# Token mixing in a two-block transformer: four edits to when side work is issued between the projections

## The chip, the cores and the metric

The kernel runs on one core of one Trainium2 chip. The time is device microseconds (us) of one execution; the kernel before was run three times, with a median of 1366.09 us (1365.25 to 1366.57). One further execution was profiled, and all rows below come from it.

## The reference, cut to what matters

There are 256 tokens of 1024 features in float32. A first block (attention, pooling, a mixture of 32 experts) is not touched by the change. The second block has two layers, and each is a token mixing and an MLP. The change lies in the token mixing:

```python
def second_block(x, positions, attn_norm_w, w_in, hgrn_lower_bounds, w_out, mlp_norm_w, w_up, w_down, final_norm_w):
    ...
    for layer in range(DEPTH_2):
        h = rms_norm_2(x, attn_norm_w[layer])
        proj = h @ w_in[layer]
        a_q, a_i, a_zf, a_zb, a_g, b_u, c_q, c_k, c_v = jnp.split(proj, SPLIT_POINTS, axis=-1)
        o_a = hgrn2_mixer(a_q, a_i, a_zf, a_zb, a_g, lb_all[layer]).astype(x.dtype)
        o_b = fourier_mixer(b_u).astype(x.dtype)
        o_c = dilated_attention_mixer(c_q, c_k, c_v, positions).astype(x.dtype)
        mixed = jnp.concatenate([o_a, o_b, o_c], axis=-1)
        x = x + mixed @ w_out[layer]
        h = rms_norm_2(x, mlp_norm_w[layer])
        x = x + jnp.square(jax.nn.relu(h @ w_up[layer])) @ w_down[layer]
    return rms_norm_2(x, final_norm_w)
```

`hgrn2_mixer` is a gated linear recurrence in both directions (4 heads of 64), `fourier_mixer` the real part of a 2-D DFT, and `dilated_attention_mixer` a softmax attention of 8 heads of 64 on rotated queries and keys, over three dilations.

## The kernel before, in words

**Products.** Every weight matrix arrives in pieces of 1 MB (four row blocks of 128 by 512 columns) on SP's queue, in the order in which they are asked for. ScalarE (ACT) rounds a piece to float32r (`wh`, line 163, with the norm's weights as scale) and VectorE (DVE) makes the rest (`wl`, line 164), two row blocks to a tile, four tiles of each. A row block then costs six matmuls of 512 columns on TensorE (PE): for each of the two token tiles hi times hi, lo times hi and hi times lo (lines 186 to 188). So a projection of 512 columns has eight row blocks, 48 matmuls (called products below) in all.

**Side steps.** A mixing layer makes six projections in the order z (gates of the recurrence), q and i (recurrence), rotary q, rotary k, v of the attention (cv), and g and u (gu). The remaining work of the mixing is written as Python generators, and each `yield` ends a side step. `tok_part` calls `bg()` after every second row block, so four times in a projection, and `bg()` advances every generator in the list `bgs` by one step. The generators are, in the order of the list:

- `turn()` (line 1434), put at the head of the list by `evac_rot` after the q and the k projection: eight PE transposes of the rotated tile `rx` and two ACT copies into `qT` or `kT`. `rx` is made from the projection's PSUM by eight DVE and four POOL (GpSimd) instructions (lines 1427 to 1432).
- `hgrn()` (line 1269): transposes of z (`pz`), then of q (`pq`), then eight levels with DVE and POOL products (lines 1329, 1333, 1365, 1366) and small matmuls (`hsm`, `diag`, `cross`). In the first layer it first lets two steps pass.
- `attention()` (line 1509), appended after the k projection: four times `scores` (head group g, token tile t): eight matmuls (`sc`), then a softmax of DVE (lines 1471, 1474, 1480), POOL (1475, 1483) and ACT (1479); then for each group `values`: two steps with eight transposes of the probabilities (`pt`) and copies of these (`pT`, one on DVE and one on ACT), and one with the products with v (`po`).
- `fourier()` (line 1517): appended after the gu projection.

After the gu projection the loop `while att in bgs: bg()` runs what is left of the attention, and then come the first half of the w_out projection with the remaining steps of `hgrn()` and `fourier()`, and its second half.

**What sets the order.** A planner places the instructions when the program is built: the place in the program is an instruction's priority, and where the planner's own durations say that an instruction is not ready, one behind it may go ahead. On the chip every engine then runs its queue in the order that was placed. All matmul outputs share eight PSUM banks.

The lines that the change touches: 200 to 206 (`tok_part`), 1272 (`hgrn`), 1434 to 1443 (`turn`), 1509 (`attention`), 1543 to 1549 (`proj`) and 1564 (the gu projection).

Of the kernel before, what the change touches and what calls it, by code (L numbers as in the profile page):

```python
# [34 lines left out]
def shape_constants():  # L35
    """Arrays that follow from the shapes alone."""
# [14 lines left out]
    # cos up to 128, then sin from 1 to 127; the other frequencies mirror these  # L51
# [25 lines left out]
def back(src):  # L77
    """src [128, n] with its columns in reverse."""
    (pstep, pn), (fs, n) = src.ap
    return bass.AP(tensor=src.tensor, offset=src.offset + (n - 1) * fs, ap=[[pstep, pn], [-fs, n]])  # L80


class Feat:
    """Features on the partitions, as a float32r pair hi + lo: a [128, 256] tile for each 128 of them."""
# [11 lines left out]
class FeatBlocks:  # L96
    """The same, a [128, 2 token tiles, 4 blocks, 128] tile for each 512 features."""
# [12 lines left out]
class Kernel:  # L110
    # the pair of experts before which the loop over crowded experts stands, and how many of its loads go ahead of the loop
# [9 lines left out]
    def add_ring(self, st, n, **kw):  # L121
        """n more slots of 8 KB a partition, last in turn, until st closes."""
        pool = st.enter_context(self.tc.tile_pool(name="ring", bufs=n, **kw, reuse_waits="tile"))
        self.wslots[self.slot:self.slot] = [pool] * n
        self.slot = (self.slot + n) % len(self.wslots)

        def drop():
            self.wslots, self.slot = [q for q in self.wslots if q is not pool], 0
        st.callback(drop)

    def load(self, src, f):
# [3 lines left out]
        # loads start in the order in which they are asked for  # L135
# [5 lines left out]
    def load_small(self, dst, src):  # L141
        """In the queue of the weights, two after each load asked for from now on."""
        self.smalls.append((dst, src))
# [12 lines left out]
    def split(self, v, g=None):  # L156
        """v [128, n] float32 -> two float32r tiles whose sum is v, or v times g's column for each half of it."""
# [13 lines left out]
    def halves(self, v, g=None):  # L171
        """A slot [128, 4, 512] as (hi, lo, offset) for each of its four row blocks; g: a column to scale each block by."""
# [6 lines left out]
    def tok_step(self, ps, hT, k, wh, wl, first, last):  # L179
        """ps[t] += h[t] @ w for one row block, token tiles stationary."""  # L180
# [9 lines left out]
    def feat_step(self, ps, hT, k, hi, lo, off, first, last):  # L190
        """Four 128-feature tiles of (h @ w)^T for one row block, weights stationary; two tiles in a bank."""
# [8 lines left out]
    def tok_part(self, ps, hT, w, kb, c0, first, last, bg=None, g=None):  # L200
        """ps[t] += h[t] @ w for four row blocks."""
        for k, hi, lo, off in self.halves(self.load_k(w, kb, c0), g):
            c = slice(off, off + 512)
            self.tok_step(ps, hT, kb + k, hi[:, c], lo[:, c], first and k == 0, last and k == 3)
            if bg and k % 2:
                bg()
# [15 lines left out]
    def sumsq(self, x, ss, junk=None):  # L222
        """ss [128, 1] = sum of x [128, n] squared."""
# [4 lines left out]
    def rsqrt(self, ss, parts, n=D):  # L228
        """rsqrt of mean + eps from the partial sums ss [128, parts]."""
# [16 lines left out]
    def transposed(self, src):  # L246
        """src [128 tokens, 512] -> psum [128, 4, 128]."""
# [5 lines left out]
    def into_hT(self, t, n):  # L253
        """A 512-wide piece of token tile t of x, transposed; a norm's weights and token scales are applied elsewhere."""
# [7 lines left out]
    def split_to(self, ft, src, name):  # L262
        """src [128, 256] float32 in SBUF or PSUM -> (hi, lo)."""
# [48 lines left out]
    def load_vectors(self, rows, which, put):  # L312
        """Vectors as rows of 128."""
# [13 lines left out]
    def turn_vectors(self, rows, first):  # L327
        """The same as columns: 128 features on the partitions."""
# [10 lines left out]
    def phase_a(self, rs):  # L339
        tc, nc, a = self.tc, self.nc, self.a  # L340
        with ExitStack() as st:
# [13 lines left out]
            # shift1, scale1  # L355
# [5 lines left out]
            # scaled tokens, transposed before the modulation is known  # L361
# [16 lines left out]
            # the first projections in four rounds of 256 features, as their shift and scale come in  # L378
# [56 lines left out]
            # relative position bias, Toeplitz in DRAM: rev[h, r] = bias(255 - r), masked beyond  # L435
# [11 lines left out]
            # behind the splits of weights that the tensor engine needs before  # L447
# [11 lines left out]
            # a head pair's results later take the place of its q and k, a pool group's that of its u  # L459
# [35 lines left out]
            # query rows run backwards within a tile, so that the bias loads with positive steps  # L495
            sm = {}

            def scores(u, t):
                """Causal softmax of heads 4g+j and 4g+j+2 (one row half of q and k each), token tile t."""
# [63 lines left out]
            def average(g):  # L563
                """Moving average over 2^(g+1) tokens less the token itself."""
# [34 lines left out]
            # the first norm of the second block also takes the weights of the first block's last one  # L599
# [5 lines left out]
            def modulations():  # L605
                """gate1 on all partitions, shift2 and scale2 as columns."""
# [65 lines left out]
            # gate2 stays in PSUM until the experts' pools are open  # L672
# [20 lines left out]
            # the last slot one token tile after the other  # L693
# [16 lines left out]
    def rotary(self, pos, tmp):  # L710
        """Rotary tables of the second block."""
# [25 lines left out]
    def bounds(self, p):  # L737
        """Lower bounds of the second layer's gates: (p0 + p1) - p0 of a softmax over the layers."""
# [22 lines left out]
    def ada_quad(self, ps, vs, ks, first, last):  # L761
        """Rows 32j.. of ps get c @ vs[j], row blocks ks[j].. of c; the four column groups run together."""
# [12 lines left out]
    def halves_cols(self, dst, mod, pt, nb):  # L775
        """dst [128, 2 chunks, nb]: mod rows as columns, groups 2i and 2i + 1 summed."""
# [3 lines left out]
    def ada_sum(self, chunk, y, first):  # L780
        """y = or += the row blocks of c @ w_ada, 128 partial sums for each of 512 columns; in four steps."""
# [11 lines left out]
    def gate_sums(self, gate, chunk, put):  # L793
        """Two chunks as a gate, the same on all partitions, a half at a time to put; summed in gate [128, 1024]."""
        nc = self.nc
        c = self.vcol["b_ada", 16] + 4 * chunk - 16
        for n in range(2):
            y = gate[:, n * 512:(n + 1) * 512]
            # a diagonal with the bias adds it to the sum over the partitions
# [23 lines left out]
    def route_piece(self, t, n, p):  # L823
        """The part of the logits that a 512-wide piece of token tile t gives."""
# [15 lines left out]
    def choose(self, p):  # L840
        """Group and experts of each token. Leaves A (experts of a token) and what the weights follow from."""
# [34 lines left out]
    def slots(self, p):  # L876
        """Rm: the slot of a token in an expert, -1 without; cnt: tokens of each expert."""
# [14 lines left out]
    def combine(self, p):  # L892
        """Weight of an expert for a token."""
# [25 lines left out]
    def phase_b(self, rs):  # L919
        tc, nc, a, misc = self.tc, self.nc, self.a, self.misc  # L920
        with ExitStack() as st:
# [3 lines left out]
            # normed tokens, hi and lo, in hT's place: [n] is a [128, 2 token tiles, 512] piece  # L925
# [22 lines left out]
            for pr in range(16):  # L948
# [30 lines left out]
                # gate and up: expert j in the column half j of the array  # L979
# [26 lines left out]
                # slot -> token matrix and combine weights of the pair  # L1006
# [34 lines left out]
            # x + gate2 * y goes into hT, its second half later  # L1041
# [10 lines left out]
    def final_norm(self, gf, junk, rc):  # L1052
        """x = norm_f(x), in two steps; rc: the token scales of this norm and the next one, together."""
# [11 lines left out]
        for t in range(2):  # L1065
            ra = self.rsqrt(ssa[t], 2)
            # mean square after the first norm: that of x * gf, times ra^2
# [9 lines left out]
    def modulate(self, dst, src, k):  # L1077
        """dst = src * a2 + s2 for row block k of the features."""
# [5 lines left out]
    def overflow(self, p, pw, comb, Rm, cnt, h2):  # L1084
        """Experts with more than 64 tokens: each further run of 64 in a turn of a loop."""
# [12 lines left out]
        # run index 96 - v8 = 32 * (turn - 1) + expert  # L1098
# [92 lines left out]
    def phase_c(self):  # L1191
        tc, nc, a = self.tc, self.nc, self.a
        with ExitStack() as st:
# [4 lines left out]
            # nothing reads what the squares leave in mT  # L1198
# [22 lines left out]
    def mix_layer(self, layer, rc, late):  # L1221
        """x += mixers(rms_norm(x)) @ w_out; hT holds x * weight, rc the token scales; late calls bring its second half.
        Returns the same for the next norm."""
        tc, nc, a = self.tc, self.nc, self.a
        with ExitStack() as st:
# [35 lines left out]
            def pairs(name, b0):  # L1261
                """Two blocks of 128 features of tk[name], transposed."""
# [6 lines left out]
            def hgrn():  # L1269
                nc.gpsimd.memset(ES, 1.0)  # L1270
                # the first layer's token scales come late
                for _ in range(0 if layer else 2):
                    yield
# [14 lines left out]
                # sums over s of score(s, t) v(s). Level h: s and t in different halves of a block of 2h, the forward  # L1288
                # direction where s is in the first half; both directions' factors lie in one tile, half by half
                # [member of the pair, pair, ...]: a member's products use one row half and need PSUM banks of their own  # L1290
                sd = p.tile([128, 2, 2, 2, 32], F32, name="sd")

                def small_mm(lv, kt, qt):
                    """Within blocks of 32; what the level doesn't cover is masked."""
# [25 lines left out]
                for lv in range(8):  # L1320
# [3 lines left out]
                    def half(x, w, h=h):  # L1324
                        """A half of each block of 2h: [128, blocks, h]"""
# [23 lines left out]
                    else:  # L1349
                        # [pair, query tile]: keys of the other tile  # L1350
# [8 lines left out]
                    if lv < 7:  # L1359
                        # whole-block products extend the exclusive, then the inclusive products  # L1360
# [9 lines left out]
                # the blocks of 32 join the same-tile scores; same tile: [key tile] blocks, other tile: [query tile] blocks  # L1370
# [138 lines left out]
            def attention():  # L1509
                for g in range(2):  # L1510
                    yield from scores(g)
# [197 lines left out]
```

## Time and profile before

| | us |
|---|---|
| median of three runs | 1366.09 |
| span of the profiled execution, first to last instruction | 1360.8 |
| what the median has beyond that span | 5.3 |
| PE busy in the span | 1280.2 (94%) |
| DVE busy | 665.8 (49%) |
| ACT busy | 510.7 (38%) |
| POOL busy | 212.8 (16%) |

For the profiled execution the page gives its span and no time of its own, so the 5.3 us are the difference to the median of the timed runs. The first layer's mixing lies at about 725 to 855 us of the span, the second layer's at about 1037 to 1167 us. An engine's times in a view are from the span's start; the time in square brackets is how long the engine stood idle before an instruction, and what ended that.

### The profile page before, as it was taken

How to read it: one execution, taken by the hardware profiler on the slowest of the kernel's cores; microseconds unless marked ns; L12 is line 12 of the kernel's file. 1: busy time of each engine (PE TensorE's matmuls, PEld its weight loads, DVE VectorE, ACT ScalarE, POOL GpSimd, SP SyncE). 2: the span in 40 equal slices, each digit the busy share in tenths (PEclk: the TensorE clock that was granted, in tenths of full speed). 3: DMA queues.
4: the chain of work that ended last, by engine and by line, in shares of the span. 5: the costliest groups of instructions: out<-in, count | busy, mean ns of one | idle time of the engine just before them, and what ended most of it. 6: DMA issues, size and time to landing. Idle time of an engine off the chain costs nothing. (4 is left out here: it accounts for less than half of the span.)

```text
span 1360.8 us, 19889 instructions
## 1 busy us (share of the span) xinstructions
PE 1280.2 (94%) x7977; PEld 874.7 (64%) x7977; DVE 665.8 (49%) x1146; ACT 510.7 (38%) x917; POOL 212.8 (16%) x280
## 2 busy tenths in 40 slices
PE   5999987899999899999998999999999999999997
PEld 3899974343333334343435777989897767899896
DVE  3797995111111111111117994655656895655554
ACT  2455423011111101010106555655555546655553
POOL 1011120000000000000004462211113463111102
PEclk9999998999999999999999899999999999999999
DMA  9997897999999699999996323556554433555540
GB/s 327 378 329 258 319 379 260 390 394 394 393 393 393 241 395 395 393 393 393 393 379 224 124 94 112 184 179 206 181 192 159 152 125 93 187 195 192 186 155 32
DMA packets 169926, 359.36 MB, mean 264 GB/s; under 512 B 9020, under 2 KB 18112, under 8 KB 169832
## 3 DMA queue, kind: packets, MB, share of 16 engines
q1 hardware_dynamic: 169288, 356.99, 73.0%
q8 instruction: 63, 1.03, 0.3%
q0 software_dynamic: 352, 1.07, 0.2%
q14 instruction: 31, 0.25, 0.1%
q10 hardware_dynamic: 192, 0.02, 0.0%
HBM read 356.99 MB, written 1.06 MB: 263 GB/s over the span
## 5 line engine op out<-in xcount | busy, mean ns | idle before, releaser
L168 DVE TENSOR_TENSOR wl<-w,wh 128x1024 fp32r<-128x1024 f32 x128 | 157.0, 1231 | 102.2 <-ACT wh L167 102.2
L167 ACT CAST wh<-w 128x1024 fp32r<-128x1024 f32 x128 | 134.0, 1050 | 143.3 <-PE up L197 64.5
L1030 PE MATMUL py<-w,actT 128*64 128x512 f32 x512 | 137.7, 606 | 14.7 <-issue 14.0
L163 ACT ACTIVATE wh<-w,vcols 128x512 fp32r<-128x512 f32 x176 | 121.3, 718 | 77.9 <-PE dn L187 34.7
L164 DVE SCALAR_TENSOR_TENSOR wl<-w,vcols,wh 128x512 fp32r<-128x512 f32 x176 | 131.2, 778 | 36.6 <-ACT wh L163 34.6
L197 PE MATMUL up<-hT,wh 128*128 128x256 f32 x512 | 142.3, 278 | 0.0
L196 PE MATMUL up<-hT,wh 128*128 128x256 f32 x512 | 142.2, 278 | 0.0
L198 PE MATMUL up<-hT,wl 128*128 128x256 f32 x512 | 142.2, 278 | 0.0
L982 PE MATMUL pg<-w,xT 128*64 128x512 f32 x512 | 129.0, 599 | 0.0
L982 PE MATMUL pu<-w,xT 128*64 128x512 f32 x512 | 126.0, 594 | 0.0
L187 PE MATMUL dn<-wh,actl 128*128 128x512 f32 x256 | 101.2, 395 | 0.0
L186 PE MATMUL dn<-wh,acth 128*128 128x512 f32 x256 | 101.2, 395 | 0.0
L188 PE MATMUL dn<-wl,acth 128*128 128x512 f32 x256 | 101.1, 396 | 0.0
L197 PEld LDWEIGHTS up<-hT,wh 128*128 128x128 f32 x512 | 96.9, 189 | 0.6
L1030 PEld LDWEIGHTS py<-w,actT 128*64 128x64 f32 x512 | 44.4, 137 | 82.0 <-issue 79.9
L196 PEld LDWEIGHTS up<-hT,wh 128*128 128x128 f32 x512 | 96.1, 188 | 0.6
L198 PEld LDWEIGHTS up<-hT,wl 128*128 128x128 f32 x512 | 96.0, 188 | 0.5 <-DVE wl L164 0.5
L1624 POOL TENSOR_TENSOR relu<-relu 128x256 f32<-128x256 f32 x64 | 53.7, 838 | 265.8 <-ACT relu L1623 265.8
L186 PE MATMUL b<-wh,hT 128*128 128x512 f32 x224 | 92.0, 411 | 0.7 <-ACT hT L259 0.7
L1035 ACT ACTIVATE yh<-py,ws 128x512 fp32r<-128x512 f32 x32 | 22.0, 687 | 184.9 <-PE py L1030 184.9
L188 PE MATMUL b<-wl,hT 128*128 128x512 f32 x224 | 88.1, 398 | 2.5 <-DVE wl L168 2.5
L187 PE MATMUL b<-wh,hT 128*128 128x512 f32 x224 | 88.3, 395 | 0.4 <-DVE hT L260 0.4
(403 smaller groups left out, 2170.5 us busy)
## 6 DMA issues: line engine op xcount, KB each, us to landing
w<-in_w_expert_gate_dram SPq DMA_DIRECT2D x64, 1024.0 KB, 14.6
w<-in_w_expert_up_dram SPq DMA_DIRECT2D x64, 1024.0 KB, 14.2
w<-in_w_expert_down_dram SPq DMA_DIRECT2D x64, 1024.0 KB, 14.0
w<-in_w_in_dram SPq DMA_DIRECT2D x40, 1024.0 KB, 8.1
w<-in_w_up_dram SPq DMA_DIRECT2D x32, 1024.0 KB, 5.4
w<-in_w_down_dram SPq DMA_DIRECT2D x32, 1024.0 KB, 5.1
w<-in_w_ada_dram SPq DMA_DIRECT2D x24, 1024.0 KB, 9.7
w<-in_w_out_dram SPq DMA_DIRECT2D x12, 1024.0 KB, 5.1
```

Of the source, the lines that this page charges most:

```text
L163: self.nc.scalar.activation(hi[:, c], v[:, c], AF.Copy, scale=g[:, i:i + 1])
L164: self.nc.vector.scalar_tensor_tensor(lo[:, c], v[:, c], g[:, i:i + 1], hi[:, c].bitcast(F32), op0=ALU.mult, op1=ALU.subtract)
L167: self.last_hi = self.nc.scalar.copy(hi, v).ins
L168: self.last_lo = self.nc.vector.tensor_tensor(lo, v, hi, op=ALU.subtract).ins
L186: nc.tensor.matmul(ps, hT.tok(0, k, t), wh, start=first, stop=False)
L187: nc.tensor.matmul(ps, hT.tok(1, k, t), wh, start=False, stop=False)
L188: nc.tensor.matmul(ps, hT.tok(0, k, t), wl, start=False, stop=last)
L196: nc.tensor.matmul(o, hi[:, c], hT.mov(0, k), start=first and m % 2 == 0, stop=False, skip_group_check=True)
L197: nc.tensor.matmul(o, hi[:, c], hT.mov(1, k), start=False, stop=False, skip_group_check=True)
L198: nc.tensor.matmul(o, lo[:, c], hT.mov(0, k), start=False, stop=last and m % 2 == 1, skip_group_check=True)
L982: nc.tensor.matmul(dst[64 * j:64 * j + 64], xT[:, k, so + 64 * j:so + 64 * j + 64], w[j][k // 4][:, k % 4], start=k == 0, stop=k == 7, til ...
L1030: nc.tensor.matmul(py[64 * j:64 * j + 64], aT[:, f, 64 * j:64 * j + 64], d[j][f // 2][:, f % 2, n * 512:(n + 1) * 512], start=f == 0, stop ...
```

## The change

Four edits in `mix_layer` and one parameter that `tok_part` and `proj` pass on; comments and docstrings go as well, which issue nothing.

- `turn()` yields once before its transposes, so that they come one side step later.
- `hgrn()` lets one more step pass at its start (three in the first layer, one in the second).
- `turn()` notes in `turned` that its tile is complete, and `attention()` yields until both are. As `turn()` stands ahead of `attention()` in the list, the first scores are issued in the step that transposes k, the second of the cv projection and not the first.
- The gu projection calls `bg()` after each of its eight row blocks and not after every second one.

```diff
-    def tok_part(self, ps, hT, w, kb, c0, first, last, bg=None, g=None):
+    def tok_part(self, ps, hT, w, kb, c0, first, last, bg=None, g=None, every=2):
...
-            if bg and k % 2:
+            if bg and k % every == every - 1:
                 bg()
...
-                for _ in range(0 if layer else 2):
+                for _ in range(1 if layer else 3):
                     yield
...
             qT, kT = f4("qT"), f4("kT")
+            turned = []
...
                     def turn():
+
+                        yield
                         for m in range(0, 4, 2):
...
                             nc.scalar.copy(dst[:, m:m + 2], ps)
+                        turned.append(dst)
                         yield
                     gens.insert(0, turn())
...
             def attention():
+                while len(turned) < 2:
+                    yield
                 for g in range(2):
                     yield from scores(g)
...
-            def proj(c0, e, late=()):
+            def proj(c0, e, late=(), every=2):
                 ps = [bank() for _ in range(2)]
-                self.tok_part(ps, hT, win, 0, c0, True, False, bg, g=gw[:, 0:4])
+                self.tok_part(ps, hT, win, 0, c0, True, False, bg, gw[:, 0:4], every)
                 for f in late:
                     f()
-                self.tok_part(ps, hT, win, 4, c0, False, True, bg, g=gw[:, 4:8])
+                self.tok_part(ps, hT, win, 4, c0, False, True, bg, gw[:, 4:8], every)
                 e(c0, ps)
...
-            proj(1024, evac_gu)
+            proj(1024, evac_gu, every=1)
```

## Rows read from the trace of the kernel before

**Rows 1.** The page: busy us, share of the span and instructions of each engine.

```profile
PE 1280.2 (94%) x7977; PEld 874.7 (64%) x7977; DVE 665.8 (49%) x1146; ACT 510.7 (38%) x917; POOL 212.8 (16%) x280
```

**Rows 2.** PE's waits: total us, times, longest; three rows 734:860, then 1040:1175.

```profile
PE prot L1440 <- POOL rx L1432: 2.9, 4, 1.1
PE pz L1266 <- ACT z L1253: 2.9, 1, 2.9
PE po L1503 <- DVE pT L1495: 1.3, 1, 1.3
...
PE prot L1440 <- POOL rx L1432: 3.6, 4, 1.1
```

**Rows 3.** DVE's waits from 749 to 810, first layer: all of them.

```profile
DVE wl L164 <- ACT wh L163: 3.0, 1, 3.0
DVE sl L1310 <- PE hsm L1303: 0.9, 1, 0.9
```

**Rows 4.** Window: length; busy of PE, PEld, DVE, ACT, POOL (count); clock; DMA.

```profile
1102.30:1119.10 16.80, 16.80 (x147) 12.14 (x146) 16.80 (x31) 9.32 (x24) 10.53 (x15) 1.00 0.34 127
```

**Rows 5.** Timeline of PE: start, us; transposes of z, first and second layer.

```profile
748.88 1.75 PE L1266 MATMUL pz<-ident,z 128*128 128x128 f32 x7 [2.92 <-ACT z L1253]
...
1057.03 1.04 PE L1266 MATMUL pz<-ident,z 128*128 128x128 f32 x8
```

**Rows 6.** Windows on PE's products: length, PE busy (count), granted clock, DMA.

```profile
750.29:756.96 6.67, 6.67 (x24) 0.85 0.46 157
774.88:781.23 6.35, 6.35 (x24) 0.90 0.49 165
1086.15:1091.94 5.79, 5.79 (x24) 1.00 0.55 169
```

**Rows 7.** Timeline of PE: last six transposes of rotated q, first and second layer.

```profile
772.81 1.54 PE L1440 MATMUL prot<-ident,rx 128*128 128x128 f32 x6 [0.73 <-POOL rx L1432]
...
1084.93 0.88 PE L1440 MATMUL prot<-ident,rx 128*128 128x128 f32 x6 [0.72 <-POOL rx L1432]
```

**Rows 8.** Groups, 1069 to 1146: count, busy us, mean ns, idle before.

```profile
L163 ACT ACTIVATE wh<-w,vcols 128x512 fp32r<-128x512 f32 x24 | 16.3, 715 | 17.4 <-PE b L187 17.3
```

**Rows 9.** Timeline of PE, second layer: the last scores and what follows.

```profile
1115.06 1.13 PE L1466 MATMUL sc<-kT,qT 64*128 64x256 f32 x8
...
1131.07 1.51 PE L1503 MATMUL po<-pT,cv 128*64 128x256 f32 x12 [1.27 <-DVE pT L1495]
1135.38 1.03 PE L1494 MATMUL pt<-ident,s 128*128 128x128 f32 x8
1136.35 1.71 PE L1356 MATMUL cross<-qt,kt 64*128 64x128 f32 x16
...
1141.25 0.64 PE L1375 MATMUL diag<-sd,ident 32*32 32x128 f32 x16
```

**Rows 10.** Timeline of POOL, second layer: softmax (L1475, L1483) and recurrence.

```profile
1112.16 0.31 POOL L1475 TENSOR_SCALAR mx<-mx 128x4 f32<-128x4 f32 x1 [3.36 <-DVE mx L1474]
...
1115.77 1.10 POOL L1311 TENSOR_TENSOR sd<-sd,sl 128x128 f32<-128x128 f32 x2
1116.82 1.89 POOL L1333 TENSOR_TENSOR kt<-hk,hES 128x256 f32<-128x256 f32 x2
...
1123.82 2.11 POOL L1483 TENSOR_SCALAR s<-s,l 128x256 f32<-128x256 f32 x4 [2.42 <-DVE l L1480]
...
1129.07 5.00 POOL L1483 TENSOR_SCALAR s<-s,l 128x256 f32<-128x256 f32 x4 [0.53 <-DVE l L1480]
```

**Rows 11.** Timeline of DVE, second layer, beside that.

```profile
1123.55 0.18 DVE L1480 RECIPROCAL l<-l 128x4 f32<-128x4 f32 x1 [2.75 <-ACT s L1479]
...
1129.20 1.22 DVE L168 TENSOR_TENSOR wl<-w,wh 128x1024 fp32r<-128x1024 f32 x1
```

**Rows 12.** Timeline of ACT, second layer: the gu projection's evacuation.

```profile
1134.10 1.28 ACT L1454 ACT_TABLE_LOAD   x1
...
1137.72 0.49 ACT L1455 ACTIVATE u<-b,rs 128x256 f32<-128x256 f32 x1
```

## The prediction

> **What bounds the kernel now.** I read the page's busy times first: PE is busy 94% of the span, DVE 49% [rows 1]. So time is won where PE stands idle, and the change must be judged by the two mixing stretches alone. The waits of PE there come next [rows 2]. In the first layer PE waits 2.9 us in four pieces for the rotated q and k (`rx`), 2.9 us for z, and 1.3 us in the products with v for a copy of the probabilities (`pT`). In the second layer it waits 3.6 us for `rx` and again 1.27 us for `pT` [rows 2, 9], and none for z: its eight transposes follow without a gap [rows 5]. The sum is 12.0 us, under 1% of the span.
>
> The reader should not stop at PE. In the middle of the second layer's mixing DVE is busy 16.80 of 16.80 us, just as PE is, and POOL 10.53 [rows 4]. In the first layer DVE pauses only twice between 749 and 810 us, 3.0 us at the start and 0.9 us later [rows 3]. So for 50 us two engines are full, and the wait for `pT` is where the second one shows. A gap closed on PE alone is not yet won.
>
> **What the change removes.** The profiled span is 1360.8 us; the median of the timed runs is 5.3 us more. I take these 5.3 us as unchanged and add the changes to the median.
>
> *z, first layer.* The transposes move behind 12 more products. 24 products take 5.79 us at full clock [rows 6], so 12 take 2.9 us and fill the 2.92 us but for some 0.2 us. The wait also costs clock: the first 24 products behind it take 6.67 us at a granted 0.85 against 5.79 us at 1.00 [rows 6], and seven transposes 1.75 us where eight take 1.04 in the second layer [rows 5]: 0.9 + 0.8 = 1.7 us, given back with the gap. Against it, z now stands closer to q: q's evacuation follows z's on ACT with a table load between (a load is 1.28 us, rows 12), and PE's transposes of q may wait for it, 0 to 1.3 us; I take 0.7. Together 2.7 + 1.7 - 0.7 = 3.7 us. What the recurrence makes of z is wanted only after q, so that the step does not delay it. In the second layer, which has no wait here, the same edit is worth nothing; were the step not covered by the q projection, it would cost one step, 2.9 us.
>
> *Rotated q and k.* With 12 products (2.9 us) put in between, the waits of at most 1.1 us [rows 2] go: 2.9 us and 3.6 us. Cover is there, since ACT's rounding of the weights stands idle 17.3 us for PE to release its buffers, so operands are ahead [rows 8]. In the first layer clock comes back too: 24 products behind the q transposes take 6.35 us, 0.56 more than at 1.00 [rows 6], and six transposes 1.54 against 0.88 us [rows 7]: 1.2 us. Sum 4.1 us in the first layer, 3.6 in the second.
>
> *`pT`.* The products with v come two row blocks of work later behind the first scores than PE's own order would allow, so this wait is either gone or part of the wait below: 1.3 us in each layer.
>
> Removed: 3.7 + 4.1 + 1.3 = 9.1 us in the first layer, 3.6 + 1.3 = 4.9 us in the second, 14.0 us in all.
>
> **What it adds.** The added wait puts each layer's four score steps one step later, and a step is again 2.9 us; with 3.6 us won before it, the second layer's scores come 0.7 us earlier than now. Behind the scores PE now has less to do before it wants their result. The last probabilities are wanted by the transposes at 1135.38 [rows 9]. In the new order 18 of gu's products (4.35 us) come behind these and no longer ahead of them, while `cross` (1.71 us, rows 9) comes ahead. PE gets there at 1135.4 - 4.9 - 4.35 + 1.7 = 1127.9 us. Now the softmax: the last scores end at 1116.19 [rows 9], the last four scalings on POOL at 1134.07 [rows 10], 17.9 us. If that length stays, the result is there at 1133.4, and PE stands 5.5 us with 18 products queued behind the transposes. So far the 17.9 us were covered by gu.
>
> Can the chain be shorter? POOL carries 1.10 + 1.89 us of the recurrence in front of it, though it stood idle 3.36 us shortly before [rows 10]; with the scores a step later against the recurrence these 3.0 us can go into that hole. Then 1130.4, a wait of 2.5 us. I add 0.4 us for ACT's copies of k, behind which the first scores now stand at once, and for PSUM (gu, `diag`, `cross` and `pt` hold two banks each, and there are eight). I take 2.9 us. The lower bound is DVE's queue: the `pT` copy that released PE at 1131.07 [rows 9], less DVE's 2.75 us idle and less 1.22 us for a piece of w_out [rows 11], is 1127.1, and with four scalings at 2.11 us [rows 10] 1129.2: 1.3 us. The upper bound is 5.5.
>
> *First layer.* PE wins 4.2 us more here, but DVE, full since 749, can give back only its 0.9 us pause [rows 3]. So 3.3 us of the lead end in the same wait: 2.9 + 3.3 = 6.2 us (bounds 1.3, if DVE reorders its weight work behind the softmax, and 5.5 + 4.2 = 9.7).
>
> *Behind gu.* Now the attention's last steps cover gu's evacuation. Afterwards only `diag` (0.64 us, rows 9) lies between gu's last product and the Fourier products, which need u: four ACT pieces like that of u, 4 x 0.49 = 2.0 us, and a table load of 1.28 us ahead of them where ACT is late [rows 12]. Less 0.64 this is 1.3 to 2.6 us, or nothing where the planner puts w_out's first products there. I take 0.8 us a layer, 1.6 us.
>
> A step for every row block issues the same side instructions, and the loads keep their order on SP; DMA is busy to a third there [rows 4], so nothing is charged. A memset of the Fourier tile on POOL, which waits until `rx` is read, comes later with the transposes; it falls into POOL's idle time.
>
> **Sum.** 14.0 - 2.9 - 6.2 - 1.6 = 3.3 us: 1366.1 - 3.3 = 1362.8 us, a span of 1357.5. At the bounds: 14.0 + 0.7 - 1.3 - 1.3 = 12.1 gives 1354.0; 14.0 - 0.6 - 5.5 - 9.7 - 5.2 = -7.0 gives 1373.1.
>
> **Rivals.**
>
> *A. The waits simply go.* The planner fills what is left with products of the next row blocks, as it put `hsm` products among the transposes before. Then PE alone counts: 14.0 to 14.7 us less, about 1352. For it: PE is 94% busy and operands are ahead [rows 1, 8]. Against it: DVE is full [rows 4], and the planner did not see the present waits.
>
> *B. The softmax keeps its length.* Waits of 5.5 and 5.5 + 3.3 = 8.8 us, and 1.6 behind gu: 14.0 - 15.9 = -1.9, 1368.0 us. For it: DVE stood 2.75 us in its queue at a reciprocal [rows 11], an order that the planner chose and may choose again.
>
> *C. Slower.* POOL's four scalings of one softmax take 2.11 us once and 5.00 us beside DVE's making of weight remainders [rows 10, 11]. In the new order the scalings fall deeper into the stretch in which DVE works on gu's and w_out's weights. If one more group takes 5.00, the chain is 2.9 us longer than now: waits of 8.4 and 11.7 us, 14.0 - 21.7 = -7.7, 1373.8 us. It decides from where the two waits exceed 14.0 - 1.6 + 2.7 = 15.1 us, a softmax chain over 18.3 us instead of 17.9. The Trainium skill, page "SBUF — State Buffer", section "Who interferes with whom", states that a DVE instruction with two SBUF inputs and a GpSimd one that reads SBUF exclude each other for a whole instruction; the 5.00 us agree with that, though no row shows such a pair by itself.
>
> *D. The edits don't do what they say.* A step is a priority for the planner and no place in a queue; if it puts scores and transposes where they were, the time stays at 1366.
>
> **How the numbers follow.** Chances: forecast 0.55 (1358.5 to 1366), A 0.15, B 0.13, C 0.12, D 0.05. A measurement of this kernel can tell about 0.2%, 2.7 us, from no change. Faster than 1363.4 are A and 0.31 of the forecast: 0.46. Within 0.2% are 0.24 of the forecast, D, and most of B (0.11): 0.40. Slower are C and the rest of B: 0.14. The range leaves out A's most and the upper part of B with C: 1356.0 to 1368.5; the forecast's own is 1358.5 to 1366.
>
> **What would show it.** Right: no wait of PE for `rx`, none over 0.3 us for z, full clock from 749 on, and in their place a wait of PE `pt` for POOL's scalings (some 3 us in the second layer, 6 in the first) and one of `f` for u. Wrong: no wait at `pt` (then A), or `sc` placed where they are now (D); a last group of scalings that ends later than 18 us after its scores means B or C. If the first layer wins as much as PE's waits there, DVE's full queue was no bound, and that step is wrong.

## The result, and the profile after

The changed kernel takes 1376.21 us (1374.37 to 1380.62), the kernel before beside it 1366.33: a ratio of 1.0083 (1.0065 to 1.0101). The forecast was 1362.8 with a range up to 1368.5: sign and size are wrong. The profiled execution takes 1374.47 us, its span 1372.7 against 1360.8.

The first view is the window of each mixing stretch, from the last transposes of x ahead of it to the first behind it. Columns: length; busy of PE, PEld, DVE, ACT, POOL (count); granted clock; DMA share; GB/s. Before:

```profile
730.60:855.50 124.90, 117.11 (x1041) 91.19 (x1040) 92.92 (x166) 71.17 (x142) 58.84 (x77) 0.97 0.41 139
1043.12:1166.93 123.81, 118.74 (x1065) 93.17 (x1064) 94.06 (x172) 70.34 (x136) 54.51 (x65) 1.00 0.40 133
```

After:

```profile
733.12:862.55 129.43, 118.67 (x1041) 90.70 (x1040) 92.34 (x166) 70.87 (x142) 55.76 (x77) 0.96 0.39 135
1050.18:1178.81 128.63, 121.86 (x1065) 95.03 (x1064) 94.91 (x172) 70.17 (x136) 51.76 (x65) 0.96 0.39 128
```

The stretches are 4.5 and 4.8 us longer, 9.4 us together. Half of that is idle time of PE (length less busy: 7.79 to 10.76 and 5.07 to 6.77, +4.7). The other half is PE's busy time, which grows by 4.7 us for exactly as many instructions, at a granted clock of 0.96 where it was 0.97 and 1.00. What the span gained beyond this (2.5 us) lies ahead of 733, in a part that the change doesn't touch; there the start of the stretch moved from 729 to 736 us between the profiles of this case. So all comparisons below use the sum of the two stretches (248.7 us before, 258.1 after) beside the medians. Each sum comes from one profiled execution, and it moves by itself too: the last section shows the same instructions of one layer taking 71.9 and 73.3 us.

The waits of PE, to be read against [rows 2] (total us, times, longest). First layer, then second:

```profile
PE sc L1470 <- DVE s L1475: 3.0, 1, 3.0
PE prot L1443 <- POOL rx L1433: 3.0, 3, 1.2
PE po L1507 <- DVE pT L1499: 1.6, 1, 1.6
PE pq L1266 <- ACT q L1258: 1.5, 2, 1.1
PE f L1529 <- ACT u L1459: 0.7, 1, 0.7
...
PE pz L1266 <- ACT z L1253: 0.2, 1, 0.2
PE sc L1470 <- DVE s L1475: 2.7, 1, 2.7
PE diag L1346 <- DVE s L1475: 1.5, 1, 1.5
PE po L1507 <- DVE pT L1499: 0.9, 1, 0.9
PE f L1529 <- ACT u L1459: 0.7, 1, 0.7
PE prot L1443 <- POOL rx L1433: 0.6, 1, 0.6
```

There is no row for `pt`, where the forecast put the new wait. In its place the score products themselves wait, and they wait for DVE's read of *other* scores. That is no operand of theirs, so what they wait for must be room in PSUM. The order on PE shows it, second layer (start, us, line, xcount, idle before and its releaser), to be held against [rows 9]:

```profile
1109.29 1.13 PE L1470 MATMUL sc<-kT,qT 64*128 64x256 f32 x8
...
1117.14 1.48 PE L1470 MATMUL sc<-kT,qT 64*128 64x256 f32 x8
...
1122.05 0.96 PE L1346 MATMUL diag<-qt,kt 64*32 64x32 f32 x64 [1.45 <-DVE s L1475]
1122.94 1.22 PE L1470 MATMUL sc<-kT,qT 64*128 64x256 f32 x2
1126.82 2.07 PE L1470 MATMUL sc<-kT,qT 64*128 64x256 f32 x6 [2.66 <-DVE s L1475]
1131.55 1.81 PE L1498 MATMUL pt<-ident,s 128*128 128x128 f32 x8
```

DVE reads the scores late, and ACT evacuates cv late (DVE, then ACT):

```profile
1116.15 1.28 DVE L1475 SCALAR_TENSOR_TENSOR s<-sc,kmix 128x512 f32<-128x512 f32 x2
...
1126.08 1.27 DVE L1475 SCALAR_TENSOR_TENSOR s<-sc,kmix 128x512 f32<-128x512 f32 x2
```

```profile
1119.01 0.51 ACT L1483 ACTIVATE s<-s,mx 128x256 f32<-128x256 f32 x1 [4.11 <-POOL mx L1479]
...
1121.00 0.66 ACT L1453 ACTIVATE cv<-b,rs 128x512 f32<-128x512 f32 x1
...
1124.45 0.51 ACT L1483 ACTIVATE s<-s,mx 128x256 f32<-128x256 f32 x1 [2.17 <-POOL mx L1479]
...
1126.43 0.67 ACT L1453 ACTIVATE cv<-b,rs 128x512 f32<-128x512 f32 x1
```

When the last scores come to PE at 1122.94, one bank is free. Counted by the order of the instructions, the other seven hold one half of cv (until 1127.10, behind exponentials that waited for POOL's negated maximum), both halves of `diag`, both of gu, and both of the third scores, which DVE reads only from 1126.08. The second bank comes with that read. The Trainium skill, page "PSUM — Partial Sum Buffer", section "Specifications (TRN2)", gives eight banks a partition; the count agrees with it. The restart is slow, too:

```profile
1126.82:1131.75 4.93, 4.93 (x13) 3.42 (x14) 4.93 (x9) 1.53 (x5) 4.81 (x9) 0.50 0.00 0
```

After 1.45 and 2.66 us of idle time TensorE was granted half its speed (1.2 GHz) for these 4.93 us: six score products and a run of six of gu cost 2.07 and 2.93 us.

### The profile page after: what moved, and what is told of

Its sections match the earlier page's. It is cut to its first block, busy times and chain, and to the rows that moved or that the text cites. A ratio compares the mean times of both kernels' runs of the same rounds, so it can differ in the third digit from the quotient of the medians.

```text
span 1372.7 us, 19906 instructions
## 1 busy us (share of the span) xinstructions
PE 1289.7 (94%) x7977; PEld 880.8 (64%) x7977; DVE 665.2 (48%) x1146; ACT 509.8 (37%) x917; POOL 206.9 (15%) x280
## 5 line engine op out<-in xcount | busy, mean ns | idle before, releaser
L186 PE MATMUL b<-wh,hT 128*128 128x512 f32 x224 | 94.1, 421 | 1.0 <-ACT hT L259 0.7
L187 PE MATMUL b<-wh,hT 128*128 128x512 f32 x224 | 89.4, 400 | 0.5 <-DVE hT L260 0.5
```

The source lines that it names most:

```text
L186: nc.tensor.matmul(ps, hT.tok(0, k, t), wh, start=first, stop=False)
L187: nc.tensor.matmul(ps, hT.tok(1, k, t), wh, start=False, stop=False)
```

## The experiments

Each was timed in five rounds beside the kernel before, and the ratio is to that kernel in the same rounds (its medians beside e1 to e18 lie between 1364.9 and 1365.9 us). The stretch sum is that of the two windows defined above.

| run | median us | ratio (95%) | stretches us |
|---|---|---|---|
| before / after | 1366.3 / 1376.2 | 1.0083 (1.0065, 1.0101) | 248.7 / 258.1 |
| e1 after, gu by two | 1368.3 | 1.0026 (1.0014, 1.0038) | 252.1 |
| e2 before, gu by one | 1374.4 | 1.0070 (1.0047, 1.0093) | 256.4 |
| e3 before, scores late | 1368.6 | 1.0021 (1.0006, 1.0036) | 251.9 |
| e4 before, z late | 1365.8 | 1.0006 (0.9992, 1.0021) | 250.1 |
| e5 e2, attention paced | 1370.4 | 1.0034 (1.0022, 1.0047) | 254.5 |
| e6 after, paced | 1371.2 | 1.0049 (1.0034, 1.0064) | 254.5 |
| e7 after, hold ahead of diag | 1368.6 | 1.0029 (1.0016, 1.0042) | 252.4 |
| e8 before, q late | 1365.5 | 0.9998 (0.9986, 1.0011) | 249.5 |
| e9 after, hold behind diag | 1375.1 | 1.0075 (1.0058, 1.0093) | 258.0 |
| e10 e3, values one later | 1371.0 | 1.0050 (1.0034, 1.0066) | 256.2 |
| e11 e3, values two later | 1370.8 | 1.0042 (1.0028, 1.0055) | 254.4 |
| e12 e11, tail beside | 1372.9 | 1.0056 (1.0038, 1.0074) | 257.8 |
| e13 e3, negation on DVE | 1365.0 | 0.9998 (0.9984, 1.0011) | 248.4 |
| e14 e13, scalings halved | 1366.4 | 1.0009 (0.9995, 1.0023) | 250.2 |
| e15 e7, as e14 | 1372.0 | 1.0043 (1.0026, 1.0059) | 254.4 |
| e16 before, as e14 | 1362.7 | 0.9982 (0.9972, 0.9992) | 246.5 |
| e17 e7, negation on DVE | 1368.4 | 1.0024 (1.0012, 1.0036) | 252.1 |
| e18 before, negation on DVE | 1361.6 | 0.9966 (0.9953, 0.9979) | 246.4 |

**Which edit loses (e1 to e4).** The change is taken apart. Theory P says that the step per row block of gu piles up PSUM banks behind the later scores; theory Q, that the later scores are the loss. e1 takes the gu edit away:

```
-            proj(1024, evac_gu, every=1)
+            proj(1024, evac_gu)
```

> The changed kernel with the gu projection's side steps back at every second row block; the other edits stay. Theory P (too many PSUM banks wanted at once: with a side step per row block of gu the last scores meet diag, cv's two unread banks, gu's two and the scores before them, PE waits 4.2 us a layer for DVE to read a scores bank and its clock falls): the waits of sc and diag for DVE's reading of scores go, and the time falls to 1358 to 1363 us. Theory Q (the scores' delay by one step is the loss: DVE reads the first scores 5.7 us late because weight work stands ahead of it): these waits stay at 2 us or more a layer or turn into waits of pt, and the time stays at 1370 us or more.

e2 is the kernel before with the gu edit alone (`every`), e3 with the attention's edit alone (the `yield` in `turn`, `turned`, and the wait for both), e4 with the recurrence's alone (`range(1 if layer else 3)`).

> The kernel before with the gu edit alone: a side step after each of gu's eight row blocks. Theory P: the scores are all issued before gu begins, so no bank of theirs is missing; what can wait is pt for the scalings and f for u (0.7 us): 1364 to 1370 us, and no wait of sc. Theory Q: no loss without the scores' delay, 1362 to 1367 us. A loss of more than 4 us would speak for a third theory: gu by one row block loses by itself, because the softmax isn't done when its probabilities are wanted.

> The kernel before with the transposes of q and k one step later and the scores waiting for both, alone; gu and the recurrence as before. Theory P: the waits for rx go (2.9 and 3.6 us), none of sc for DVE comes, 1360 to 1365 us. Theory Q: slower than before by 3 us or more, 1369 to 1374 us, with DVE reading the first scores over 4 us late.

> The kernel before with the recurrence's first step one step later, alone. Both theories: the first layer's wait for z (2.92 us) becomes a wait of pq for q of about 1.5 us and the clock does not fall behind it; 2 to 4 us faster, 1362 to 1364.5 us, if DVE's full queue in the first layer does not take the lead back. If it does: 1365 to 1366.5 us.

Against the kernel before, the stretches grow by 7.6 us with the gu edit, 3.2 with the scores' and 1.3 with z's. The last is not told from nothing, neither by the times of e4 nor by a stretch that moves by 1.4 us by itself. The parts don't add up to the whole (12.1 against 9.4 us); taking the gu edit out of the changed kernel gives 6.0 us back (e1). e1 and e3 end at 1368.3 and 1368.6 us, between what P and Q say: both edits lose. That gu by row blocks loses by itself is in neither P nor Q, but it is the third theory that e2's expectation names. In e2 nothing waits at `sc`, but the probabilities are wanted a run of six products earlier at each step; second layer:

```profile
PE pt L1497 <- DVE s L1474: 1.4, 1, 1.4
PE pt L1497 <- POOL s L1486: 0.5, 2, 0.4
PE po L1506 <- ACT pT L1498: 0.4, 1, 0.4
```

The first row ends with DVE's read of the last scores, so again with a free bank (the transposes start at 1129.03, the read began at 1128.30). But POOL's scalings, which they need too, last until 1128.72, so most of that wait would have been there with a bank free. The clock falls behind these waits:

```profile
1127.00:1132.00 5.00, 3.30 (x10) 2.71 (x11) 3.54 (x7) 3.08 (x10) 2.58 (x6) 0.62 0.00 2
1132.00:1137.00 5.00, 5.00 (x49) 4.01 (x47) 4.54 (x8) 2.73 (x11) 3.71 (x7) 0.70 0.00 0
```

Busy time times what was not granted is 3.30 x 0.38 + 5.00 x 0.30 = 2.8 us: more than the waits. In e1 the wait of `sc` is gone, and the wait that was forecast appears at `pt` for POOL's scalings, 4.1 us in the second layer and 3.2 in the first; e3 has the same one (4.3 and 4.2) and only 0.6 us left of the wait for `rx` in either layer. e4 shows why z won nothing: its wait falls from 2.9 to 0.2 us in the first layer, but the wait for `rx` grows from 2.9 to 5.6 and `pq` waits 1.5. DVE, full there [rows 3], takes the lead back: in e4 an instruction of the recurrence, at 770.94 after 0.62 us of waiting for POOL, stands ahead of the rotation in its queue.

**Is it the short runs of products (e5, e6)?** Theory W says that the loss comes from what is wanted early, theory R that runs of six lose by themselves. e5 is e2 with the attention's steps at every second row block, as before (it also has one `yield` ahead of the loop); e6 does it in the changed kernel:

```
                 for g in range(2):
-                    yield from values(g)
+                    for _ in values(g):
+                        yield
+                        yield
```

> The kernel before with the side step behind each row block of gu, but with the attention's steps held to every second one, so that the products with v stand where they stood; only the recurrence's last steps come closer together. Theory W (a step per row block costs because the probabilities are wanted six products earlier at each step, and TensorE's waits then cost clock too): the loss of 9 us that the edit alone made goes, 1364 to 1368 us, no wait of pt over 1 us and from the first score to f 39.5 to 40.5 us as before. Theory R (runs of six products between side steps cost by themselves): 1369 to 1374 us, the clock below 1.00 again without a wait at pt. Theory P (PSUM banks): diag and cross hold their banks earlier here, so a wait of pt or po for a bank would show; 1367 to 1372.

> The changed kernel with the attention's steps behind the last scores held to every second row block; the last scores stay behind gu's first row block. Theory W: the scores' own lateness stays, the values are wanted as in the run with gu by two, so 1367 to 1370 us, a wait at pt of 3 to 4 us in each layer in place of those at sc and diag. Theory P (the last scores, put at gu's first row block, find no free bank): the wait of sc for the read of the scores stays at 2.5 to 3 us in each layer, and the time at 1372 to 1377 us.

Both theories miss a part. e5's 1370.4 us lies in theory R's range, and the clock falls without a wait at `pt` in the second layer, as R has it. e5 still loses 5.8 us in the stretches, with less idle time of PE than before from the first score to f in the second layer (1.0 against 1.45 us). What is early now is the recurrence: `cross` is asked for ahead of its `kt`, and its second bank is still held by a `pt` that ACT has not copied:

```profile
1134.95 1.16 PE L1356 MATMUL cross<-qt,kt 64*128 64x128 f32 x8 [0.28 <-POOL kt L1333]
1136.84 1.16 PE L1356 MATMUL cross<-qt,kt 64*128 64x128 f32 x8 [0.73 <-ACT pT L1498]
```

Behind these 1.0 us the windows 1135 to 1140 and 1140 to 1145 were granted 0.80 and 0.86, which are means of both levels (1137.92 to 1140.70 had 0.52); the first layer has the same two waits and 0.90 and 0.76. The kernel before stood 1.27 us at `po` [rows 9] and kept 1.00. The runs of six themselves cost little: from the first score to `f` in the second layer, PE's busy time times the granted clock is 41.0 x 0.94 = 38.5 us in e5 and 38.1 x 1.00 before. So most of the loss is clock behind early, short waits. But 1.4 of the 5.8 us come in the second layer before gu begins, and so ahead of anything that e5 edits (last section), and why one wait costs clock and another doesn't, no run settles. e6 keeps its 3.0 us at `sc` in both layers, as theory P expects, yet ends at 1371.2 us, nearer to theory W.

**PSUM or DVE's queue (e7, e9).** In e7 the recurrence is held until the last scores are issued, ahead of the products that take `diag`'s banks. e9 is its control: the same lines behind these products, so that DVE is relieved of the same work and only the place of these products, and with it the banks, differs.

```
+                    while lv == 5 and len(probs[0]) + len(probs[1]) < 4:
+                        yield
                     if lv < 5:
```

> The changed kernel with the recurrence's sixth level (the first that takes diag's two banks) held until the last scores are issued: two banks more are free when these come. Theory P: the wait of sc goes below 0.7 us, 1370 to 1373 us. Theory W: the banks only move the wait: what sc no longer waits, pt waits, and the time stays at 1374 to 1378 us.

> The control to the run that held the recurrence ahead of diag: the changed kernel with the same hold put behind diag's first products, so that DVE is relieved of the same recurrence work at the same time, but diag's two PSUM banks are taken as in the changed kernel. Theory P (banks): the wait of sc for the read of the scores is back at 2.5 to 3.0 us in each layer and the time at 1373 to 1378 us. Rival, DVE's queue (it was the recurrence's work ahead of the read that made the wait): as the run with the hold ahead of diag, sc below 1.5 us, 1367 to 1370 us.

Second layer of e7:

```profile
PE sc L1472 <- DVE s L1477: 1.4, 1, 1.4
PE pt L1500 <- POOL s L1489: 1.1, 1, 1.1
PE diag L1348 <- DVE s L1477: 1.0, 1, 1.0
```

and of e9:

```profile
PE sc L1472 <- DVE s L1477: 2.8, 1, 2.8
PE diag L1346 <- DVE s L1477: 1.4, 1, 1.4
PE po L1509 <- ACT pT L1501: 0.8, 1, 0.8
```

In the first layer `sc` doesn't wait at all in e7 and waits 3.0 us in e9. DVE's read of the third scores, e7 and then e9:

```profile
1122.65 1.28 DVE L1477 SCALAR_TENSOR_TENSOR s<-sc,kmix 128x512 f32<-128x512 f32 x2
1125.63 1.28 DVE L1477 SCALAR_TENSOR_TENSOR s<-sc,kmix 128x512 f32<-128x512 f32 x2
```

The layer's first scores start at 1106.00 and 1108.98, so this read comes 16.65 us behind them in both: DVE's queue up to it is not what differs. The control is the changed kernel again (258.0 us), e7 is 5.6 us shorter, and faster than theory P's own range, though P's sign, `sc` below 0.7 us, holds in the first layer alone. This shows the cause of the larger part: two banks taken by `diag` ahead of the last scores. In e7 it is the second half of `diag` that waits for the read, 1.0 us.

**Can the lead on the queries be kept, or the values be moved (e8, e10 to e12)?** e8 delays only the queries' transposes; e10 and e11 put one and two `yield` ahead of the values in e3; e12 adds the recurrence's last steps and the Fourier products beside the attention's.

> The kernel before with the transposes of the rotated queries alone one step later, scores and keys as before. Theory W: nothing that is wanted early is delayed, so q's half of the rx waits (1.7 us in the second layer, 1.4 in the first) is won with some clock: 1361 to 1363.5 us. Rival, DVE is full: what PE wins stands again at the next wait for DVE or POOL (the keys' rx, or pT): 1364.5 to 1366.5 us, with those waits longer by the same amount.

> The kernel before with the later transposes and scores alone, and the first probabilities' transposes too one step later, 12 products further. Theory W (the loss of that edit is that the values were not moved with the scores): of the wait at pt, 4.2 us in each layer, 1 to 2 us are left, its clock comes back, and with the rx waits gone it is 1362 to 1366 us. Rival (what is not waited there is waited behind gu, where no products are left to cover it): new waits of pt or po behind gu of 2 to 3 us a layer, 1366 to 1370 us.

> The same with the values two steps later, 24 products. Theory W: no wait of pt over 0.5 us, 1360 to 1365 us. Rival: five of the attention's six last steps now lie behind gu, each waits for the copy of the one before: 3 to 4 us of waits a layer, 1366 to 1371 us.

> The same again, with the recurrence's last steps and the Fourier products issued beside the attention's last steps and not behind them. Theory W: as the run without, or up to 1.5 us less, 1360 to 1364 us. Rival: this is the cover that was missing, so it is 2 to 4 us less than the run without.

Four misses for W. e8 and e11 end where the rival says, e10 just above it; in e12 the rival misses too, for it is 2.1 us slower than e11 and not 2 to 4 faster, with a new wait of 1.9 us for g in each layer. In e8 the `rx` wait stays 3.7 us in the second layer, now all with the keys: the products put in between help only until the next wait for DVE, which is full, and POOL. In e3's line the wait only moves: 4.2 us at `pt`, in e10 4.0 at `cross` for ACT's `pT`, in e11 and e12 6.1 at `pt` for DVE's `pT`. The softmax ends no earlier: its last scalings start 30.3 us behind the second layer's first scores in e3, e10 and e11.

**What makes the softmax long (e13 to e18).** In e11 ACT's last exponentials stood idle 4.6 us for the negated maximum, which stands behind other scalings in POOL's queue; e3 has the same order, second layer, POOL:

```profile
1128.05 0.71 POOL L1479 TENSOR_SCALAR mx<-mx 128x4 f32<-128x4 f32 x1 [2.31 <-DVE mx L1478]
1128.74 3.81 POOL L1487 TENSOR_SCALAR s<-s,l 128x256 f32<-128x256 f32 x4
1132.53 1.42 POOL L1333 TENSOR_TENSOR kt<-hk,hES 128x256 f32<-128x256 f32 x2
1133.93 2.80 POOL L1487 TENSOR_SCALAR s<-s,l 128x256 f32<-128x256 f32 x4
1136.70 0.19 POOL L1479 TENSOR_SCALAR mx<-mx 128x4 f32<-128x4 f32 x1
1139.38 2.81 POOL L1487 TENSOR_SCALAR s<-s,l 128x256 f32<-128x256 f32 x4 [2.48 <-DVE l L1484]
```

Theory N: take this one small instruction out of POOL's queue (e13, e17, e18); e14 to e16 also move two of four scalings to ACT.

```
-                    nc.gpsimd.tensor_scalar(mx, mx, -1.0, 0.0, op0=ALU.mult, op1=ALU.add)
+                    nc.vector.tensor_scalar(mx, mx, -1.0, None, op0=ALU.mult)
...
+                            if j:
+                                nc.scalar.activation(s[:, j, i], s[:, j, i], AF.Copy, scale=l[:, j, i:i + 1])
...
```

> The kernel before with the later transposes and scores alone, the negation of the softmax's maximum done on DVE and not on POOL. Theory N (POOL's order makes the chain long: the negation stands behind another softmax's scalings): the last probabilities come 2 to 3 us earlier, the waits at pt fall from 4.2 to 1 to 2.5 us in each layer, 1362 to 1366 us. Rival, DVE's queue: the negation waits as long on DVE as on POOL, waits at pt 3.5 to 5 us, 1367 to 1370 us.

> The same, and two of each softmax's four scalings on ACT and not on POOL. Theory N: another 1 to 1.5 us off each softmax, no wait at pt over 1 us, 1359 to 1364 us. Rival: ACT's scalings stand behind its roundings of weights and nothing is won on e13's time.

> The changed kernel with the recurrence held ahead of diag until the last scores are issued, and with the negation on DVE and half of the scalings on ACT. Theory N with P: of the waits that the hold left (sc 1.4, pt 1.1, diag 1.0 us in the second layer) the one at pt goes, the others, for DVE's reading of the scores, stay: 1364 to 1368 us. Rival (the chain was not what bounds here): as the hold alone, 1367 to 1370 us.

> The kernel before with the negation on DVE and half of the scalings on ACT, nothing of the change. Its softmax chain was covered by gu but for 1.3 us in each layer (the wait of po for pT). Theory N: that wait goes, 1362 to 1365 us, and e14 is 2 to 3 us below it by the rx waits. Rival (no gain here, since DVE and PE are full): 1364 to 1367 us, with e14 not below it.

> The changed kernel with the recurrence held ahead of diag and the negation on DVE; all scalings stay on POOL. If PSUM banks and POOL's order are the two causes and add up: 1364 to 1367 us, the two mixing stretches some 9 us shorter than in the changed kernel, no wait at pt over 0.5 us. Rival (they share the same wait, DVE's read of the scores being left when one goes): 1367 to 1372 us, diag and sc still waiting 2 us and more together in the second layer.

> The kernel before with the negation on DVE alone. If the chain was covered by gu in the kernel before but for the wait at pT: 1.3 us a layer go, 1362 to 1364.5 us. Rival: as before, 1364.5 to 1366.5 us, the gain of the run with both having come from the scalings on ACT.

e13 gives back all that e3 lost (251.9 to 248.4 us). Its last scalings start 28.7 us after the layer's first scores (1134.68 less 1105.99), 30.3 in e3 (1139.38 less 1109.11): 1.6 us, and the waits at `pt` fall from 4.3 to 2.0 us, in three pieces of at most 0.9. Scalings on ACT win nothing on this (e14; e16 beside e18), and with `diag` held they lose (e15, slower than both its ranges and 3.6 us behind e17; why was not found). With `diag` held the negation gives nothing (e17, 0.3 us): `sc` still waits 1.3 us for DVE's read in the second layer and `diag` 1.4 us in the first. So the two gains don't add, and what is left of both is a wait for that read. In the kernel before, the third softmax's negation starts 4.0 us behind its maximum (1121.21 against 1117.25), in e18 0.8 us (1120.79 against 1120.00). The negation alone makes e18 the fastest of all, 0.34% below before, and the only waits over 0.3 us left in its second layer's stretch are

```profile
PE prot L1440 <- POOL rx L1432: 3.0, 4, 1.1
PE pt L1494 <- POOL s L1483: 0.4, 1, 0.4
```

e13 is e18 with the later scores: 2.0 us longer in the stretches, although 3.0 - 0.6 us of the wait for `rx` are gone in the second layer; its time is 3.4 us longer. The later order loses even with the shorter chain.

## Why the prediction was wrong

Measured by its own steps, the sum of -3.3 us was made of -0.4 us of waits (11.1 removed, 10.7 added) and -2.9 of clock given back. The stretches show +4.7 of idle time and +4.7 of slower products. So the larger error, 7.6 of 12.7 us, is clock, of which some 1.4 us can come and go without an edit.

- **A step for every row block, "nothing is charged".** This step failed. The edit alone costs 7.6 us (e2). The text did count the 18 products that no longer stand ahead of the last transposes, but for all other side steps it counted only instructions and DMAs, and not that each wants its operand and its PSUM banks six products earlier.
- **"I add 0.4 us for ACT's copies of k ... and for PSUM".** The term was mis-sized: the two banks of `diag` alone measured 5.6 us over both layers (e7 against e9), the clock behind the waits included. The sentence counted who holds two banks, but not the unread scores and the unevacuated cv, whose readers stand in the queues of DVE and ACT.
- **New waits cost only their length.** The forecast let removed waits give clock back and charged none to the new ones. After waits of 1.45 and 2.66 us, 4.93 us ran at 0.50; e2 lost 2.8 us of clock in 10 us.
- **The wait at `pt`, 2.9 and 6.2 us.** As a mechanism it is there once gu goes by two (4.1 and 3.2 in e1; 4.3 and 4.2 in e3). In the changed kernel it stands earlier, at `sc` and `diag` (4.2 and 3.0). The order of the layers was wrong. So was the shorter chain: the forecast took 3.0 us off the 17.9, but from the last scores to the last scaling the second layer measures 18.3 us in e1 and e3, which is rival B by the forecast's own sign (over 18 us). (In the changed kernel it is 12.9 us, since the last scores themselves come late.) The forecast saw POOL's place in the chain (rivals B and C), but looked for the price in the scalings; the negation between them was 1.6 us of it (e13).
- **Rotated q and k.** Right in the second layer (3.6 to 0.6 us) and, alone, in the first (0.6 in e3). In the changed kernel the first layer keeps 3.0 us: z's later step pushes DVE's work on it into that of the rotation (5.6 in e4). The two terms were added as if they were independent, while the text itself had DVE full there [rows 3]. The wait at `pT` did not go either (1.3 to 1.6 and 0.9).
- **z.** The wait fell to 0.2 us, as forecast, and `pq` waited 1.5 and not 0.7; the term of 3.7 us came to nothing (e4).
- **Behind gu.** Right: 0.7 us a layer against 0.8.

Rival C forecast 1373.8 us, the nearest time, but by one more group of scalings of 5.00 us; in the changed kernel no group takes that long (5.81 us for two together, then 1.84 and 2.80, second layer). Its nearness is luck. Open stays what is left of the loss in e17, 3.4 us: `sc` or `diag` waits for DVE's read of the scores there, and a run that moves this read ahead in DVE's queue was not made.

## What to carry to other kernels

Before side work is moved closer together, count for each PSUM bank who reads it last and what stands in that reader's queue; a bank is held until the read, not until the product. Where several engines are full, a wait that goes on one of them comes back at the next one, often at a worse place, so look for the small in-order instruction that the chain hangs on (here one of 0.2 to 0.6 us on POOL, worth 0.34%) before reordering the large ones. Charge a new wait with the clock that may fall behind it. Compare stretches as well as whole times, since they leave out what moves elsewhere (7 us ahead of them here), but learn first how far a stretch moves by itself: here 1.4 us, so that the 1.3 us of e4 say nothing.

## What was not expected of the hardware

Two waits of PE with 2.1 us of products between them were followed by 4.93 us at a granted 0.50, while one of 1.27 us at `po` in the kernel before left it at 1.00. In e5 waits of 0.28 and 0.73 us, 1.16 us apart, were followed by 0.80 and 0.86 in one layer, 0.90 and 0.76 in the other: which wait costs clock could not be told from its length.

Nor does the same wait always cost the same. Up to the second layer's last scores nothing is edited in e2 and e5 that before has otherwise, and PE is idle for 3.6 us in all three. The first scores, behind waits of 0.9 and 0.9 us for `rx`, in before and in e5:

```profile
1102.24 1.18 PE L1466 MATMUL sc<-kT,qT 64*128 64x256 f32 x8
1108.92 2.00 PE L1469 MATMUL sc<-kT,qT 64*128 64x256 f32 x8
```

From the start of the stretch to the last scores, before takes 71.94 us (1043.12 to 1115.06), e2 71.87 and e5 73.33. These 1.4 us are clock alone, and no edit made them.
